# Three projection units instead of two beside the arriving input, with places of their own for their second weight halves

## The chip, the cores and the metric

The kernel runs on one NeuronCore of a Trainium2 chip. Five engines work side by side, each through its own list of instructions in order, and wait for one another by semaphores: TensorE (PE, matrix products; PEld is its loading of the stationary operand), VectorE (DVE), ScalarE (ACT), GpSimd (POOL), and SyncE (SP), which here only starts transfers (DMAs) from memory. The metric is the device time of one execution in microseconds (us); lower is better. Three runs of the kernel before gave 1511.23, 1511.27 and 1512.3 us, a median of 1511.27 us.

## The reference

One layer of a hybrid encoder trunk on x of 256 tokens by 2048 features, in float32. The part at issue is the very first: RMS norm of x, then one wide projection, whose first columns are the queries and keys of an attention with four heads of 128.

```python
u = _rms_norm(x, norm_mix_pre[l])           # x / rms(x) * gain
proj = u @ w_in                              # w_in: 2048 x 12580
sb, fox, rw, gates = _split(proj, ...)
q_a, k_a, v_a = _split(sb, (SB_WIDTH,) * 3)  # 512 columns each: four heads of 128
...                                          # attentions, time mixing, gates, output projection
x = x + _rms_norm(mix, norm_mix_post[l])
hdn = jnp.square(jax.nn.relu(_rms_norm(x, norm_mlp_pre[l]) @ w_mlp_up[l]))
x = x + _rms_norm(hdn @ w_mlp_down[l], norm_mlp_post[l])
```

## The kernel before

**Products in split form.** Float32 operands are cut into a rounded high part and the remainder as low part; ACT makes the high part by a copy, DVE the low part by a subtraction. A product then is high times (high, low) and low times high. For the features of x this gives a tile `xpk` of 128 x 512 (256 tokens high, 256 low) for each of 16 groups of 128 features, with the gain of the norm multiplied in. The factor 1/rms is left out at first and multiplied into the results later (`scaled`), so that the products need not wait for the norm.

**Units.** A unit is 128 output columns. Its weights are 2048 x 128, stored as two blocks of 128 x 1024 (512 KB): the first half holds feature groups 0 to 7, the second 8 to 15. Blocks come in the order of the array `wst`, so unit u has blocks 2u and 2u+1. Each block lands in a tile `raw` (tag `raw`, three places), is cut into `whi` (ACT) and `wlo` (DVE; three places each), and used by 8 products with the high part (128 x 512) and 8 with the low part (128 x 256). A unit adds up in one of four PSUM tiles `gps`.

**The ordinary loop.** `unit` (with `wnext`, `wraw` and `wsplit`) does one unit after another: load a block, cut it, multiply; the weights of the next block are made while TensorE works on the present one.

**The beginning.** x comes from memory in eight pieces of two feature groups (256 KB, `xload`), so TensorE cannot have all of xpk at once. For this time an order written out by hand holds on PE, ACT and DVE (`tc.manual_schedule`): two units, u = 0 and 1, are worked on together, feature group by feature group, as the pieces land. `part` cuts half a first block (512 columns), `xsplit` one feature group of x; `high` and `low` are the products; `whole` cuts a second block. SP issues all loads from one list, and an entry that waits holds back all behind it. The four raw blocks lie in four places: three of the tag `raw`, the fourth in a buffer of the tag `m`, which is used much later otherwise. Cut weights lie in the ordinary places of `whi` and `wlo`.

**After the beginning.** From here PE's order is still the written one, while ACT and DVE are ordered by the framework's scheduler. Units 2 to 7 follow in the ordinary loop (L191, L195 and L197 are their products). Between them ACT squares x (`square`, eight times 128 x 512, result in the tile `A6` of the tag `b6`), DVE adds the squares up (seven times), and behind the fifth unit TensorE sums them over the partitions (`norm`, L433). Then 1/rms is made, and the normed x is cut again for the later units.

Of the kernel before, what the change touches and what calls it, by code (L numbers as in the profile page):

```python
# [11 lines left out]
F32 = mybir.dt.float32  # L12
F32R = mybir.dt.float32r
AF = mybir.ActivationFunctionType
ALU = mybir.AluOpType
# [3 lines left out]
T = 256  # L19
# [4 lines left out]
HALF = 1024  # L24
# [28 lines left out]
def hybrid_block(ctx, tc, xt, x, gains, params, consts, lora, gup, wst, out):  # L53
    nc = tc.nc
    V, A, G, PE = nc.vector, nc.scalar, nc.gpsimd, nc.tensor

    cpool = ctx.enter_context(tc.tile_pool(name="cpool", bufs=1))
    wpool = ctx.enter_context(tc.tile_pool(name="wpool", bufs=1))
# [90 lines left out]
    wpos = [0]  # L149
# [5 lines left out]
    wq = []  # L155
# [4 lines left out]
    def wraw(n=None):  # L160
        raw = wpool.tile([128, HALF], F32, tag="raw", name=nm("raw"), bufs=3)
        rawdma[0] = nc.sync.dma_start(out=raw, in_=wst[wpos[0] if n is None else n])
        if n is None:
            wpos[0] = jump.get(wpos[0], wpos[0] + 1)
        return raw
# [4 lines left out]
    def wsplit(raw, n=None, now=True):  # L170
        hl = home[0](n) if home[0] else None
        hi, lo = hl or (wpool.tile([128, HALF], F32R, tag=t, name=nm(t), bufs=3) for t in ("whi", "wlo"))
        A.activation(hi, raw, AF.Copy)  # L173
        wq.append((hi, lo))
        low = lambda: V.tensor_tensor(lo, raw, hi.bitcast(F32), ALU.subtract)  # L175
        return low() if now else low
# [96 lines left out]
    rp = p1.enter_context(tc.tile_pool(name="rp", bufs=1))  # L273
# [17 lines left out]
    def xload(a, b):  # L291
        nc.sync.dma_start(out=X0[:, a:b, :], in_=xt[:, a:b, :])


    raws = {n: wpool.tile([128, HALF], F32, tag="raw", name=nm("raw"), bufs=3) for n in (0, 2)}
    for c in (0, 512):
        for n in (0, 2):
            nc.sync.dma_start(out=raws[n][:, c:c + 512], in_=wst[n][:, c:c + 512])
# [21 lines left out]
    ps = mps()  # L320
# [16 lines left out]

    def high(u, *ks):
        for k in ks:
            PE.matmul(qb[u], w[u, k // 8][0][:, k % 8 * 128:k % 8 * 128 + 128], xpk[k], start=k == 0, stop=False)  # L340

    def low(u, *ks):
        for k in ks:
            PE.matmul(qb[u][:, 0:T], w[u, k // 8][1][:, k % 8 * 128:k % 8 * 128 + 128], xpk[k][:, 0:T], start=False,
                      stop=k == 15)

    qb = [gps() for _ in range(2)]
    w = {(u, 0): [wpool.tile([128, HALF], F32R, tag=t, name=nm(t), bufs=3) for t in ("whi", "wlo")] for u in range(2)}

    def part(u, c, lo):  # L350
        c = slice(c, c + 512)
        hi, raw = w[u, 0][0][:, c], raws[2 * u][:, c]
        if lo:
            V.tensor_tensor(w[u, 0][1][:, c], raw, hi.bitcast(F32), ALU.subtract)
        else:
            A.activation(hi, raw, AF.Copy)

    def both(u, *ks):
        high(u, *ks)
        low(u, *ks)  # L360

    for c in (0, 512):
        k = c // 128
        part(0, c, False)
        xsplit(k)
        xsplit(k + 1)
        part(1, c, False)
        high(0, k, k + 1)
        high(1, k, k + 1)
        part(0, c, True)  # L370
        if c == 0:
            part(1, c, True)
        low(0, k, k + 1)
        xsplit(k + 2)
        xsplit(k + 3)
        if c:
            part(1, c, True)
        low(1, k, k + 1)
        both(0, k + 2, k + 3)
        both(1, k + 2, k + 3)  # L380

    def whole(n):
        later = wsplit(raws.pop(n), None, False)
        return wq.pop(), later

    w[0, 1], later = whole(1)
    xsplit(8)
    xsplit(9)
    later()
    both(0, 8, 9)  # L390
    xsplit(10)
    xsplit(11)
    both(0, 10, 11)
    w[1, 1], later = whole(3)
    later()
    both(1, 8, 9, 10, 11)
    for k in (12, 14):
        xsplit(k)
        xsplit(k + 1)
        both(0, k, k + 1)  # L400
        both(1, k, k + 1)
# [14 lines left out]
    side.append(lambda: const(ones, consts[:, 128:128 + NR]))  # L416
    side.append(rounded)
    side.append(lambda: const(con, consts[:, 128 + NR:]))
    wpos[0] = 4
    rstd = rp.tile([128, T], F32, tag="cs", name="rstd1", bufs=1)  # L420

    def square(i):
        xf = X0[:, 2 * i:2 * i + 2, :]
        b = 2 + 2 * (i % 2) if i else 0
        with tc.issue_after(behind[0].ins):
            A.activation(A6[:, b:b + 2, :], xf, AF.Square)
        if i:
            V.tensor_tensor(A6[:, 0:2, :], A6[:, 0:2, :], A6[:, b:b + 2, :], ALU.add)

    def norm():  # L430
        ps = mps()
        for i in range(2):
            PE.matmul(ps[:, 0:T], C("ones"), A6[:, i, :], start=i == 0, stop=i == 1)  # L433
        ms, t = tmp(), tmp()
# [37 lines left out]
    def later(i):  # L472
        normed(9 + i)
        if i < 5:
            scaled(i)
# [493 lines left out]
    for br in ("sb", "fox"):  # L969
        for s in ("q", "k"):  # L970
# [3 lines left out]
            for h in range(4):  # L974
                ps = unit(upk)
                t = g1()
# [5 lines left out]
        for i, nme, n in ((0, "zx", 128), (1, "zy", 128)) if br == "fox" else ((2, "zz", 36),):  # L982
            ps = unit(upk)
# [39 lines left out]
    for g in range(4):  # L1023
        m = rp.tile([128, 2, 512], F32, tag="m", name=nm("m"), bufs=4)
# [170 lines left out]
    low = more(False)  # L1195
# [312 lines left out]
    for g in range(4):  # L1508
        gs = slice(512 * g, 512 * g + 512)
        for tt, ps in enumerate(tok(hp, 4 if g == 3 else 1)):  # L1510
# [8 lines left out]
            if g == 3:  # L1519
                for c, w in (0, 512), (512, 512), (1024, 512), (1536, 256), (1792, 256):  # L1520
# [3 lines left out]
                        out=out[tt * 128:tt * 128 + 128, cs], in_=x1[tt][:, cs])  # L1524
# [125 lines left out]
```

## Time and profile before

| what | value |
|---|---|
| median of three runs | 1511.27 us |
| the profiled execution | 1512.76 us |
| its span in the trace | 1510.9 us |
| granted TensorE clock | 0.998 |
| busy in the span | PE 1492.3 us, PEld 1252.7, DVE 1207.6, ACT 939.4, POOL 94.6 |
| the two units done together: first product, end | 5.83 us, 21.46 us |
| the third unit (ordinary loop) | 21.46 to 27.05 us |
| the products of the norm | 38.23 us |

The profile's times count from the start of the span. A timeline row gives start, duration, engine, line, operation, result and operands, shape and how many; in square brackets stands the idle time of the engine just before it and what ended it. A transfer is issued by SP (rows SPq), and a view of the transfers gives size and time from issue to landing; the landing counts when the last of the 16 DMA engines is done.

### The profile page before, as it was taken

What the parts mean: (1) busy time and instruction counts of PE and PEld (TensorE: products, weight loads), DVE (VectorE), ACT (ScalarE), POOL (GpSimd) and SP (SyncE); (2) the same over time, 40 slices, a digit from 0 to 9 for tenths busy, and PEclk for the clock granted to TensorE, in tenths of its full rate; (3) what the DMA queues carried; (4) which work ended last, traced back from release to release, by engine and by line L of the source; (5) the groups of instructions that cost most, each with busy time, mean ns of one, the idle gap of its engine ahead of it and who ended that gap; (6) DMA issues with size and microseconds to landing.
All of it is one profiled execution on the core that took longest, in us unless ns stands there. A gap on an engine that the chain in (4) does not pass through costs nothing.

```text
span 1510.9 us, 22695 instructions
## 1 busy us (share of the span) xinstructions
PE 1492.3 (99%) x8384; PEld 1252.7 (83%) x8384; DVE 1207.6 (80%) x1673; ACT 939.4 (62%) x1433; POOL 94.6 (6%) x151
## 2 busy tenths in 40 slices
PE   9999999999999999999999999999999999999997
PEld 7888888887787887778888988888888888888886
DVE  7875679895678896476656778999899989999996
ACT  7665677545676445564445767677667666766663
POOL 0031003000002000000000000000000000000000
PEclk9999999999999999999999999999999999999999
DMA  7645455455444455355675758879888888889874
GB/s 266 196 168 182 141 180 162 148 179 187 134 170 166 155 190 174 127 182 193 214 245 172 253 178 252 251 220 287 258 262 235 222 274 240 270 265 255 251 222 150
DMA packets 104687, 312.71 MB, mean 207 GB/s; under 512 B 10240, under 2 KB 12288, under 8 KB 104576
## 3 DMA queue, kind: packets, MB, share of 16 engines
q1 hardware_dynamic: 93968, 279.87, 55.1%
q0 software_dynamic: 8064, 29.36, 10.4%
q10 hardware_dynamic: 2544, 2.03, 0.5%
q8 instruction: 66, 1.08, 0.3%
q14 instruction: 45, 0.37, 0.1%
HBM read 279.77 MB, written 2.10 MB: 187 GB/s over the span
## 4 chain that ended last, share of the span: by engine, by line
PE 94%; DVE 2%; issue 1%; ACT 1%; DMA 1%; DVEq 0%; POOLq 0%; POOL 0%; ACTq 0%; SPq 0%
PE gps L235 26%; PE gps L191 23%; PE gps L195 13%; PE gps L220 7%; PE mps L1368 3%; PE mps L1370 3%; PE mps L1369 3%; PE gps L1370 2%; PE gps L1368 2%; PE gps L1369 2%; PE gps L197 2%; DVE wlo L175 1%; PE mps L777 1%; PE gps L1157 1%; DMA raw<-in_wst_dram 1%
## 5 line engine op out<-in xcount | busy, mean ns | idle before, releaser
L175 DVE TENSOR_TENSOR wlo<-raw,whi 128x1024 fp32r<-128x1024 f32 x576 | 697.0, 1220 | 160.5 <-ACT whi L173 149.2
L173 ACT ACTIVATE whi<-raw 128x1024 fp32r<-128x1024 f32 x576 | 603.9, 1057 | 251.9 <-PE gps L235 85.8
L191 PE MATMUL gps<-pk,whi 128*128 128x512 f32 x1479 | 375.3, 392 | 0.5 <-DVE tmp L1286 0.3
L191 PEld LDWEIGHTS gps<-pk,whi 128*128 128x128 f32 x1479 | 274.4, 188 | 56.1 <-ACT whi L173 0.9
L235 PE MATMUL gps<-whi,pk 128*128 128x512 f32 x1004 | 254.8, 393 | 1.4 <-ACT whi L173 1.3
L195 PEld LDWEIGHTS gps<-pk,wlo 128*128 128x128 f32 x1582 | 215.6, 190 | 15.2 <-DVE wlo L175 0.3
L235 PEld LDWEIGHTS gps<-whi,pk 128*128 128x128 f32 x1004 | 186.1, 188 | 42.6 <-ACT whi L173 2.2
L195 PE MATMUL gps<-pk,wlo 128*128 128x256 f32 x1582 | 221.0, 282 | 0.0
L235 PE MATMUL gps<-wlo,pk 128*128 128x512 f32 x502 | 137.8, 393 | 1.7 <-DVE wlo L175 1.7
L235 PEld LDWEIGHTS gps<-wlo,pk 128*128 128x128 f32 x502 | 93.2, 188 | 22.4 <-DVE wlo L175 2.9
L1368 PE MATMUL mps<-whi,fm 128*128 128x512 f32 x224 | 88.6, 396 | 1.9 <-ACT whi L173 1.7
L1285 ACT ACTIVATE tmp<-gps 128x256 f32<-128x256 f32 x64 | 24.6, 384 | 102.9 <-PE gps L197 101.0
L1369 PE MATMUL mps<-whi,fm 128*128 128x512 f32 x224 | 87.7, 392 | 0.0
L1370 PE MATMUL mps<-wlo,fm 128*128 128x512 f32 x224 | 87.4, 390 | 0.0
L1348 POOL DMA_DIRECT2D raw<-raw x56 | 48.8, 872 | 572.4 <-DVE raw L1345 271.9
L1345 DVE TENSOR_TENSOR raw<-raw,raw 128x1024 f32<-128x1024 f32 x56 | 68.4, 1221 | 0.8
L1368 PE MATMUL gps<-whi,fm 128*128 128x512 f32 x168 | 65.9, 392 | 0.0
L1370 PE MATMUL gps<-wlo,fm 128*128 128x512 f32 x168 | 65.8, 391 | 0.0
L1369 PE MATMUL gps<-whi,fm 128*128 128x512 f32 x168 | 65.5, 390 | 0.0
L220 PE MATMUL gps<-whi,pk 128*128 128x512 f32 x224 | 60.7, 393 | 0.0
L1368 PEld LDWEIGHTS mps<-whi,fm 128*128 128x128 f32 x224 | 42.4, 189 | 10.0 <-ACT whi L173 4.0
L1370 PEld LDWEIGHTS mps<-wlo,fm 128*128 128x128 f32 x224 | 42.1, 188 | 9.5
(346 smaller groups left out, 1725.1 us busy)
## 6 DMA issues: line engine op xcount, KB each, us to landing
raw<-in_wst_dram SPq DMA_DIRECT2D x516, 512.0 KB, 4.4
raw<-raw POOLq DMA_DIRECT2D x56, 512.0 KB, 7.3
x<-in_xt_dram SPq DMA_DIRECT2D x8, 256.0 KB, 6.8
x<-in_x_dram SPq DMA_DIRECT2D x8, 256.0 KB, 5.1
raw<-in_wst_dram SPq DMA_DIRECT2D x4, 256.0 KB, 4.8
g<-in_gains_dram SPq DMA_DIRECT2D x4, 256.0 KB, 5.0
pk<-in_gains_dram SPq DMA_DIRECT2D x4, 256.0 KB, 6.9
out_dram<-x SPq DMA_DIRECT2D x4, 256.0 KB, 2.8
```

The costliest lines, as they stand in the source:

```text
L173: A.activation(hi, raw, AF.Copy)
L175: low = lambda: V.tensor_tensor(lo, raw, hi.bitcast(F32), ALU.subtract)
L191: PE.matmul(ps, hi[:, i * 128:i * 128 + 128], pks[i], start=first and i == 0, stop=False)
L195: PE.matmul(ps[:, 0:T], lo[:, i * 128:i * 128 + 128], pks[i][:, 0:T], start=False, stop=False)
L197: PE.matmul(ps, hi[:, (n - 1) * 128:n * 128], pks[n - 1], start=False, stop=True)
L220: PE.matmul(ps[tt], pks[k][:, c:c + 128], w[:, (k - k0) * 512:(k - k0) * 512 + 512], start=k == 0 and part == 0 and w is hl[0], stop=w is ...
L235: PE.matmul(ps[tt], pks[k][:, c:c + 128], w[:, (k - k0) * 512:(k - k0) * 512 + 512], start=k == 0 and part == 0 and w is hl[0], stop=False)
L1345: V.tensor_tensor(R[d, a], R[d, a], R[d, b], ALU.add)
L1348: G.dma_start(out=R[d, a], in_=R[d, b], accum_op=ALU.add)
L1368: PE.matmul(Q[f], a, w, start=d == d0 and i == 0, stop=False)
L1369: PE.matmul(Q[f], b, w, start=False, stop=False)
L1370: PE.matmul(Q[f], a, wl, start=False, stop=d == dn and i == 1)
```

## The change

Three units instead of two share the arriving pieces of x. The loads of the first halves of units 0, 1 and 2 are cut into two pieces of 512 columns each and interleaved with the pieces of x. They fill the three places of the tag `raw`. The three second halves (blocks 1, 3 and 5) are then loaded by `wraw` into the same three places, each followed by a piece of x, and their cut parts do not go to `whi` and `wlo` but to six tiles of their own: four of the tag `m`, one of `b6` and one of `Ti`. So `A6`, which is the only other tile of the tag `b6` at this stage, is taken after the group and not before it. The ordinary loop begins with unit 3 at block 6; the third unit is no longer done by it.

```diff
-    A6 = rp.tile([128, 6, T], F32, tag="b6", name="a6", bufs=1)
...
-    raws = {n: wpool.tile([128, HALF], F32, tag="raw", name=nm("raw"), bufs=3) for n in (0, 2)}
-    for c in (0, 512):
-        for n in (0, 2):
-            nc.sync.dma_start(out=raws[n][:, c:c + 512], in_=wst[n][:, c:c + 512])
-            xload(c // 128 + n, c // 128 + n + 2)
-    raws[1] = wraw(1)
-    xload(8, 10)
-    xload(10, 12)
-
-    raws[3] = rp.tile([128, 2, 512], F32, tag="m", name="raw3", bufs=4).rearrange("p a b -> p (a b)")
-    nc.sync.dma_start(out=raws[3], in_=wst[3])
-    xload(12, 14)
+    raws = {u: wpool.tile([128, HALF], F32, tag="raw", name=nm("raw"), bufs=3) for u in range(3)}
+
+    def wload(u, c):
+        nc.sync.dma_start(out=raws[u][:, c:c + 512], in_=wst[2 * u][:, c:c + 512])
...
+    seconds = []
+    for u in range(3):
+        seconds.append(wraw(2 * u + 1))
+        xload(8 + 2 * u, 10 + 2 * u)
     xload(14, 16)
...
+    more2 = [rp.tile([128, HALF], F32R, tag=t, name=nm("w2"), bufs=n) for t, n in
+             (("m", 4), ("m", 4), ("m", 4), ("m", 4), ("b6", 1), ("Ti", 1))]
...
+    def whole(u):
+        w[u, 1] = more2[2 * u:2 * u + 2]
+        A.activation(w[u, 1][0], seconds[u], AF.Copy)
+        return lambda: V.tensor_tensor(w[u, 1][1], seconds[u], w[u, 1][0].bitcast(F32), ALU.subtract)
...
+    part(2, 512, False)
+    part(2, 512, True)
+    both(1, 4, 5, 6, 7)
+    lo0 = whole(0)
+    lo0()
+    two(8)
+    both(2, 4, 5, 6, 7)
+    both(0, 8, 9)
+    lo1 = whole(1)
+    lo1()
+    two(10)
+    both(0, 10, 11)
+    both(1, 8, 9, 10, 11)
+    lo2 = whole(2)
+    lo2()
+    two(12)
+    both(2, 8, 9, 10, 11)
+    two(14)
+    for k in (12, 14):
+        for u in range(3):
+            both(u, k, k + 1)
...
-    wpos[0] = 4
+    wpos[0] = 6
+    A6 = rp.tile([128, 6, T], F32, tag="b6", name="a6", bufs=1)
...
-        ps = qb[h] if h < 2 else unit(xpk)
+        ps = qb[h] if h < 3 else unit(xpk)
```

How instructions stand now, at three places. The first is SP's list of loads at the start. Before, from the third load of weights on (`raw_88` and `raw_89` are the first halves of units 0 and 1, `raw_98` and `raw_102` the second halves, `x_82` is x, 128 x 512 is one piece of 256 KB):

```order
L298 DMA raw_88<-in_wst_dram 128x512
L292 DMA x_82<-in_xt_dram 128x512
L298 DMA raw_89<-in_wst_dram 128x512
L292 DMA x_82<-in_xt_dram 128x512 [waits DMAHW0_49]
L162 DMA raw_98<-in_wst_dram 128x1024 [waits DMAHW1_49]
L292 DMA x_82<-in_xt_dram 128x512 [waits DMAHW2_49]
L292 DMA x_82<-in_xt_dram 128x512 [waits DMAHW3_49]
L305 DMA raw_102<-in_wst_dram 128x1024 [waits DMAHW4_49]
```

Now, from the same third piece on (`raw_87`, `raw_88`, `raw_89` are the first halves of units 0, 1, 2; `raw_100`, `raw_103`, `raw_106` the second halves):

```order
L297 DMA raw_87<-in_wst_dram 128x512
L291 DMA x_82<-in_xt_dram 128x512
L297 DMA raw_88<-in_wst_dram 128x512 [waits DMAHW0_49]
L291 DMA x_82<-in_xt_dram 128x512 [waits DMAHW1_49]
L297 DMA raw_89<-in_wst_dram 128x512 [waits DMAHW2_49]
L162 DMA raw_100<-in_wst_dram 128x1024 [waits DMAHW6_49,DMAHW3_49,DVE_49]
L291 DMA x_82<-in_xt_dram 128x512 [waits DMAHW4_49]
L162 DMA raw_103<-in_wst_dram 128x1024 [waits DMAHW5_49,DMAHW0_49,DVE_49]
L291 DMA x_82<-in_xt_dram 128x512
L162 DMA raw_106<-in_wst_dram 128x1024 [waits DMAHW7_49,DMAHW2_49,DVE_49]
L291 DMA x_82<-in_xt_dram 128x512
```

Each second half now waits for DVE (DVE_49), which it did not before, and every later piece of x stands behind such a load.

The second place is DVE's list where the second halves come in. Before (`wlo_130` is the low part of unit 1's first half, `wlo_196` and `wlo_220` those of the second halves):

```order
L354 TENSOR_TENSOR wlo_130<-raw_89,whi_129 128x512 [waits DMAHW7_49]
L260 SCALAR_TENSOR_TENSOR xpk_198<-x_82,par,xpk_198 128x256 [waits DMAHW2_49,Activation_49]
L260 SCALAR_TENSOR_TENSOR xpk_201<-x_82,par,xpk_201 128x256 [waits Activation_49]
L175 TENSOR_TENSOR wlo_196<-raw_98,whi_195 128x1024 [waits DMAHW1_49]
L260 SCALAR_TENSOR_TENSOR xpk_209<-x_82,par,xpk_209 128x256 [waits DMAHW3_49,Activation_49]
L260 SCALAR_TENSOR_TENSOR pk_212<-x_82,par,pk_212 128x256 [waits Activation_49]
L175 TENSOR_TENSOR wlo_220<-raw_102,whi_219 128x1024 [waits DMAHW4_49,PE_49,Activation_49]
```

Now (`wlo_133` and `wlo_137` are low parts of first halves, `w_19_139` and `w_21_141` those of second halves in places of their own):

```order
L362 TENSOR_TENSOR wlo_133<-raw_87,whi_132 128x512 [waits DMAHW6_49,Activation_49]
L260 SCALAR_TENSOR_TENSOR xpk_188<-x_82,par,xpk_188 128x256 [waits DMAHW7_49,Activation_49]
L260 SCALAR_TENSOR_TENSOR xpk_191<-x_82,par,xpk_191 128x256 [waits Activation_49]
L362 TENSOR_TENSOR wlo_135<-raw_88,whi_134 128x512 [waits DMAHW0_49,Activation_49]
L260 SCALAR_TENSOR_TENSOR xpk_200<-x_82,par,xpk_200 128x256 [waits DMAHW1_49,Activation_49]
L260 SCALAR_TENSOR_TENSOR xpk_203<-x_82,par,xpk_203 128x256 [waits Activation_49]
L362 TENSOR_TENSOR wlo_137<-raw_89,whi_136 128x512 [waits DMAHW2_49,Activation_49]
L377 TENSOR_TENSOR w_19_139<-raw_100,w_18_138 128x1024 [waits DMAHW3_49,Activation_49]
L260 SCALAR_TENSOR_TENSOR xpk_222<-x_82,par,xpk_222 128x256 [waits DMAHW4_49,Activation_49]
L260 SCALAR_TENSOR_TENSOR xpk_225<-x_82,par,xpk_225 128x256 [waits Activation_49]
L377 TENSOR_TENSOR w_21_141<-raw_103,w_20_140 128x1024 [waits DMAHW5_49,Activation_49]
```

The low part of a second half stood behind the two feature groups that arrived with it and now stands ahead of them; the first low part in the list, `wlo_133`, is what frees the place of `raw_87`.

The third place is DVE's list behind the group. Before, the additions of squares (`a_83`) began ahead of the end of the two units, whose sums are taken over by L250:

```order
L260 SCALAR_TENSOR_TENSOR pk_248<-x_82,par,pk_248 128x256 [waits Activation_49]
L428 TENSOR_TENSOR a_83<-a_83 128x512 [waits Activation_49]
L175 TENSOR_TENSOR wlo_293<-raw_290,whi_292 128x1024 [waits DMAHW7_49,PE_49,Activation_49]
L428 TENSOR_TENSOR a_83<-a_83 128x512 [waits DVE_49,Activation_49]
L250 TENSOR_TENSOR g_48_281<-gps_125,tmp_282 128x256 [waits Activation_49]
```

Now the seven additions (`a_310`) all stand behind the three sums, the last of them between the two low parts of the sixth unit (`wlo_441`, `wlo_480`):

```order
L250 TENSOR_TENSOR g_60_337<-gps_131,tmp_338 128x256 [waits Activation_49]
L450 TENSOR_TENSOR a_310<-a_310 128x512 [waits DVE_49,Activation_49] x2
L175 TENSOR_TENSOR wlo_419<-raw_416,whi_418 128x1024 [waits DMAHW0_49,PE_49,Activation_49]
L450 TENSOR_TENSOR a_310<-a_310 128x512 [waits DVE_49,Activation_49] x3
L250 TENSOR_TENSOR g_72_403<-gps_348,tmp_404 128x256 [waits Activation_49]
L450 TENSOR_TENSOR a_310<-a_310 128x512 [waits DVE_49,Activation_49]
L175 TENSOR_TENSOR wlo_441<-raw_438,whi_440 128x1024 [waits DMAHW1_49,Activation_49]
L450 TENSOR_TENSOR a_310<-a_310 128x512 [waits DVE_49,Activation_49]
L175 TENSOR_TENSOR wlo_480<-raw_477,whi_479 128x1024 [waits DMAHW2_49,PE_49,Activation_49]
```

Behind the norm the order of ACT, DVE, POOL, SP and PE is the same as before.

More of the change, by code (lines that the diff above doesn't have):

```diff
@@ L292, in xload @@
         nc.sync.dma_start(out=X0[:, a:b, :], in_=xt[:, a:b, :])
-    raws = {n: wpool.tile([128, HALF], F32, tag="raw", name=nm("raw"), bufs=3) for n in (0, 2)}
-    for c in (0, 512):
-        for n in (0, 2):
-            nc.sync.dma_start(out=raws[n][:, c:c + 512], in_=wst[n][:, c:c + 512])
-            xload(c // 128 + n, c // 128 + n + 2)
-    raws[1] = wraw(1)
-    xload(8, 10)
-    xload(10, 12)
-    raws[3] = rp.tile([128, 2, 512], F32, tag="m", name="raw3", bufs=4).rearrange("p a b -> p (a b)")
-    nc.sync.dma_start(out=raws[3], in_=wst[3])
-    xload(12, 14)
+    raws = {u: wpool.tile([128, HALF], F32, tag="raw", name=nm("raw"), bufs=3) for u in range(3)}
+    def wload(u, c):
+        nc.sync.dma_start(out=raws[u][:, c:c + 512], in_=wst[2 * u][:, c:c + 512])
+    wload(0, 0)
+    xload(0, 2)
+    wload(1, 0)
+    wload(2, 0)
+    xload(2, 4)
+    wload(0, 512)
+    xload(4, 6)
+    wload(1, 512)
+    xload(6, 8)
+    wload(2, 512)
+    seconds = []
+    for u in range(3):
+        seconds.append(wraw(2 * u + 1))
+        xload(8 + 2 * u, 10 + 2 * u)
     xload(14, 16)
@@ L345, in low @@
                       stop=k == 15)
-    qb = [gps() for _ in range(2)]
-    w = {(u, 0): [wpool.tile([128, HALF], F32R, tag=t, name=nm(t), bufs=3) for t in ("whi", "wlo")] for u in range(2)}
+    qb = [gps() for _ in range(3)]
+    w = {(u, 0): [wpool.tile([128, HALF], F32R, tag=t, name=nm(t), bufs=3) for t in ("whi", "wlo")] for u in range(3)}
+    more2 = [rp.tile([128, HALF], F32R, tag=t, name=nm("w2"), bufs=n) for t, n in
+             (("m", 4), ("m", 4), ("m", 4), ("m", 4), ("b6", 1), ("Ti", 1))]
     def part(u, c, lo):
         c = slice(c, c + 512)
-        hi, raw = w[u, 0][0][:, c], raws[2 * u][:, c]
+        hi, raw = w[u, 0][0][:, c], raws[u][:, c]
         if lo:
@@ L360, in both, with two @@
         low(u, *ks)
-    for c in (0, 512):
-        k = c // 128
-        part(0, c, False)
+    def two(k):
         xsplit(k)
         xsplit(k + 1)
[L367 to L389, printed above, removed]
+    def whole(u):
+        w[u, 1] = more2[2 * u:2 * u + 2]
+        A.activation(w[u, 1][0], seconds[u], AF.Copy)
+        return lambda: V.tensor_tensor(w[u, 1][1], seconds[u], w[u, 1][0].bitcast(F32), ALU.subtract)
+    part(0, 0, False)
+    two(0)
+    part(0, 0, True)
+    part(1, 0, False)
+    high(0, 0, 1)
+    part(1, 0, True)
+    high(1, 0, 1)
+    part(2, 0, False)
+    low(0, 0, 1)
+    low(1, 0, 1)
+    part(2, 0, True)
+    both(2, 0, 1)
+    two(2)
+    for u in range(3):
+        both(u, 2, 3)
+    part(0, 512, False)
+    part(0, 512, True)
+    two(4)
+    part(1, 512, False)
+    part(1, 512, True)
+    both(0, 4, 5)
+    two(6)
+    both(0, 6, 7)
+    part(2, 512, False)
[5 more added lines that the diff above has]
+    both(2, 4, 5, 6, 7)
     both(0, 8, 9)
-    xsplit(10)
-    xsplit(11)
+    lo1 = whole(1)
+    lo1()
+    two(10)
     both(0, 10, 11)
-    w[1, 1], later = whole(3)
-    later()
     both(1, 8, 9, 10, 11)
+    lo2 = whole(2)
[3 more added lines that the diff above has]
+    two(14)
     for k in (12, 14):
[L398 to L401, printed above, removed]
+        for u in range(3):
+            both(u, k, k + 1)
     order.__exit__(None, None, None)
```

## Prediction

> **What bounds the kernel now.** I read the page's shares first, then the busy time by stage, with cuts at the two borders that the change moves: the end of the two units done together and the end of the third.
>
> ```profile
> span 1510.9 us, 22695 instructions
> PE 1492.3 (99%) x8384; PEld 1252.7 (83%) x8384; DVE 1207.6 (80%) x1673; ACT 939.4 (62%) x1433; POOL 94.6 (6%) x151
> ...
> 0.00:21.46 21.46, 18.14 (x76) 13.69 (x77) 13.89 (x28) 15.91 (x31) 0.76 (x12) 1.00 0.85 301
> 21.46:27.05 5.59, 5.59 (x34) 4.92 (x33) 5.18 (x8) 4.73 (x8) 0.00 (x0) 1.00 0.65 209
> 27.05:1510.90 1483.85, 1468.59 (x8277) 1234.11 (x8275) 1188.49 (x1638) 918.79 (x1396) 93.85 (x139) 1.00 0.66 206
> ```
>
> TensorE is the bound: busy 1492.3 of 1510.9 us, and without a gap in the third unit, which takes 5.59 us there. All units have the same products, so the only thing to win is idle time ahead of 21.46. TensorE's timeline shows it:
>
> ```profile
> 5.83 1.36 PE L340 MATMUL gps<-xpk,whi 128*128 128x512 f32 x4
> 8.84 0.90 PE L340 MATMUL gps<-xpk,whi 128*128 128x512 f32 x2 [0.90 <-DVE xpk L260]
> 13.28 0.51 PE L344 MATMUL gps<-xpk,wlo 128*128 128x256 f32 x2 [0.80 <-DVE wlo L354]
> 21.46 2.00 PE L191 MATMUL gps<-xpk,whi 128*128 128x512 f32 x8
> 23.30 1.12 PE L195 MATMUL gps<-xpk,wlo 128*128 128x256 f32 x8
> 24.25 0.86 PE L191 MATMUL gps<-xpk,whi 128*128 128x512 f32 x3
> 27.05 2.00 PE L191 MATMUL gps<-xpk,whi 128*128 128x512 f32 x8
> 38.23 1.02 PE L433 MATMUL mps<-a,cr 128*128 128x256 f32 x4
> ```
>
> Eight high products issue in 1.84 us (21.46 to 23.30), eight low ones in 0.95: 0.23 and 0.12 each, so 0.70 for a pair of feature groups in one unit. Two units without waits would end at 5.83 + 2 x 5.59 = 17.01; they end at 21.46. So 4.45 us are lost to waits, and that is the most the change can win. Its mark is 27.05, where three units are done now. If three units end at E, the kernel moves by E - 27.05, as long as TensorE then runs on without a new gap.
>
> What the waits hang on is the arrival of the pieces. The issues, then four of their landings (size, us from issue to landing):
>
> ```profile
> 1.65 0.42 SPq L298 DMA_DIRECT2D raw<-in_wst_dram  x1
> 2.59 0.43 SPq L298 DMA_DIRECT2D raw<-in_wst_dram  x1
> 3.54 0.43 SPq L298 DMA_DIRECT2D raw<-in_wst_dram  x1
> 4.54 0.73 SPq L162 DMA_DIRECT2D raw<-in_wst_dram  x1
> ...
> raw<-in_wst_dram SPq DMA_DIRECT2D x1, 256.0 KB, 3.7
> raw<-in_wst_dram SPq DMA_DIRECT2D x1, 256.0 KB, 5.8
> raw<-in_wst_dram SPq DMA_DIRECT2D x1, 256.0 KB, 6.9
> raw<-in_wst_dram SPq DMA_DIRECT2D x1, 512.0 KB, 7.8
> ```
>
> The third piece of 256 KB lands at 1.65 + 3.7 = 5.4, the fifth at 2.59 + 5.8 = 8.4, the seventh at 10.4, the second half at 12.3. ACT's waits give the fourth and the sixth, since it starts on x as it lands:
>
> ```profile
> 7.75 0.91 ACT L259 ACTIVATE xpk<-x,par 128x256 fp32r<-128x256 f32 x2 [1.58 <-DMA x<-in_xt_dram]
> 9.80 0.91 ACT L259 ACTIVATE xpk<-x,par 128x256 fp32r<-128x256 f32 x2 [0.62 <-DMA x<-in_xt_dram]
> 10.62 0.61 ACT L356 ACTIVATE whi<-raw 128x512 fp32r<-128x512 f32 x1
> 12.35 1.06 ACT L173 ACTIVATE whi<-raw 128x1024 fp32r<-128x1024 f32 x1 [0.32 <-DMA raw<-in_wst_dram]
> 11.14 0.68 DVE L354 TENSOR_TENSOR wlo<-raw,whi 128x512 fp32r<-128x512 f32 x1
> 11.74 0.87 DVE L260 SCALAR_TENSOR_TENSOR xpk<-x,par,xpk 128x256 fp32r<-128x256 f32 x2
> 14.65 1.22 DVE L175 TENSOR_TENSOR wlo<-raw,whi 128x1024 fp32r<-128x1024 f32 x1
> 15.78 0.48 DVE L260 SCALAR_TENSOR_TENSOR xpk<-x,par,xpk 128x256 fp32r<-128x256 f32 x1
> ```
>
> So: fourth 7.7, fifth 8.4, sixth 9.8, seventh 10.4. The second half, two sizes behind the eighth piece, lands 1.9 us after the seventh: 0.64 for each 256 KB while the queue is full. The rows also price the cutting: a half of a first block 0.61 on ACT and 0.68 on DVE, a block 1.06 and 1.22 (the next starts 1.13 after it), two feature groups 0.91 and 0.88.
>
> **The change, part by part.**
>
> *First halves of three units.* The queue's first ten pieces are now, in order: weights 0, x 0-1, weights 1, weights 2, x 2-3, weights 0, x 4-5, weights 1, x 6-7, weights 2 (0, 1, 2: the unit). Same sizes, so I put them at the landings above: weights 2 at 7.7, x 2-3 at 8.4, the second piece of weights 0 at 9.8, x 4-5 at 10.4, then 11.1, 11.7, 12.4. Against before, x comes one place later. TensorE starts at 5.83 as before, ends units 0 and 1 of groups 0-1 at 7.7, waits 0.8 for weights 2 (ACT 7.76 to 8.37) and 0.3 for their low part; groups 2-3 (x landed 8.4, ACT to 9.3, DVE to 9.9, in which the low part of weights 2 stands ahead) cost two waits of 0.17, groups 6-7 (DVE 13.0 and 13.4) 0.57 and 0.17. With 0.5 at weights 1 and the first groups the loss is 2.6, and half of the work, 8.4 us, is done at 5.83 + 8.4 + 2.6 = 16.8.
>
> *Second halves.* A second half now goes into the place of a first half, so SP issues it only when DVE has cut that one. For unit 0: landed 9.8, ACT to 10.4, DVE to 11.14, issue 11.2; before, SP issued the first of them at 4.54, with no wait on DVE. Units 1 and 2 in the same way: DVE is done with their first halves at 12.6 and 14.0. Behind each waits a piece of x, up to the last at 14.8. By 12.4 all that was queued has landed, so the queue runs dry and the flight from issue to landing, hidden before, shows. Its price stands where the loads come alone:
>
> ```profile
> raw<-in_wst_dram SPq DMA_DIRECT2D x14, 512.0 KB, 3.8
> ...
> raw<-in_wst_dram SPq DMA_DIRECT2D x1, 512.0 KB, 3.2
> ...
> raw<-in_wst_dram SPq DMA_DIRECT2D x1, 512.0 KB, 5.0
> ```
>
> These are the 14 block loads issued from 20 to 60 us, and two single ones, at 49.35 and at 21.14. The middle is 3.8, the ends 3.2 and 5.0. I take 3.8: the first second half lands at 15.0. The rest follows at 0.64 per 256 KB, because it is issued in time: x 8-9 at 15.65, second half of unit 1 at 16.9, x 10-11 at 17.6, unit 2 at 18.8, x 12-13 at 19.5, x 14-15 at 20.1.
>
> [...]
>
> *The chain behind it.* ACT cuts unit 0's second half from 15.05 to 16.1. DVE works its list in order: low part 16.14 to 17.36, groups 8 and 9 to 17.76 and 18.16, low part of unit 1 (ACT done 18.0) to 19.30, groups 10 and 11 to 19.70 and 20.10. TensorE, done with first halves at 16.8, waits 1.1 + 0.17 for groups 8 and 9 and 1.1 + 0.17 for 10 and 11. After group 11 (20.10, and 0.15 to start) it has left: one high and two low products (0.47), groups 8-11 of units 1 and 2 (2.8), groups 12-15 of three units (6 x 0.70 = 4.2). Group 15 is cut at 22.8, in time. E = 20.25 + 7.4 = 27.65.
>
> *Work that grows.* Unit 2's first half is cut in two pieces (ACT 2 x 0.61 for 1.06, DVE 2 x 0.68 for 1.22, one more DMA). On DVE this lies in the chain, and I counted it. POOL has none of it.
>
> *Squares behind the group.* A6 is free only when unit 2's last product is done. Before, additions ran up to here, 7 us ahead of the norm's products:
>
> ```profile
> 19.30 0.69 DVE L428 TENSOR_TENSOR a<-a 128x512 f32<-128x512 f32 x1
> 21.64 0.42 DVE L250 TENSOR_TENSOR g<-gps,tmp 128x256 f32<-128x256 f32 x1
> 30.55 0.68 DVE L428 TENSOR_TENSOR a<-a 128x512 f32<-128x512 f32 x1
> ```
>
> Now DVE has, between E and the norm (two units, 11.18 us later, as 38.23 is after 27.05): four sums of 0.42, three low parts of 1.22, seven additions of 0.69 = 10.2 us. It begins with some of it before E. I cost this at nothing; the cover is these two units, and only about 1 us of it is spare. If a low part in this list comes late, the norm's products wait, at most 1.5 us by that list plus an ACT copy ahead of it.
>
> *Later.* The order behind the norm is unchanged, so the shift stays.
>
> *The sum.* Waits lost before 4.45, now 2.6 + 2.45 = 5.05: +0.6 us on the profiled span of 1510.9, which makes 1511.5. That execution took 1512.76, 1.49 above the median of 1511.27, so the median goes to 1511.9. The loss at the queue eats what sharing x wins. Ends of the unknowns: the flight from 3.2 to 5.0 gives E 27.0 to 28.8. The landings four to ten hang on a slow stage early on (the fourth piece 2.3 us behind the third, against 0.64 later); a us less there makes E a us earlier, 0.5 more is as likely. Together E 26.0 to 29.3, 1510.2 to 1513.5.
>
> **The rivals.** *The overlap works as written:* second halves come so early that TensorE never waits after 5.83: E = 5.83 + 3 x 5.59 = 22.6, -4.45, 1506.8. For it: the queue moved a block in 1.3 us while full. Against: three waits of SP on DVE, and the first half's own waits of 2.6.
>
> *The second halves fly as long as those of the full queue:* 7.1 to 7.8 us, not 3.8 (the row at 4.54 had 7.8). Place: SP's first load that waits on DVE. E = 27.65 + 3.3 to 4.0, slower by 3.9 to 4.6, 1515.2 to 1515.9. It decides from a flight of 6.2 on, where E passes 30.1. Against: by the landings above some six pieces stood ahead of that row, here hardly one does. For: all landings are those of the slowest engine, and the load at 21.14 took 5.0 with an empty queue.
>
> *The norm comes late:* DVE's list of 10.2 us does not fit: up to 1.5 us more, 1513.4, still within 0.2%.
>
> **How the numbers follow.** 0.2% is 3.0 us, about what a measurement of this kernel can tell from no change. The forecast (E 26.0 to 29.3) 0.75; the late norm 0.04, also no change; the long flight 0.14, slower; the full overlap 0.07, faster. The time is the forecast's, 1511.9, its own range 1510.2 to 1513.5. For 8 in 10 the range must take in part of the long flight: 1509.8 to 1515.4.
>
> **What would show it.** SP's first load of 512 KB issued at about 11.2, behind a wait on DVE; ACT's first cut of a whole block at 15.0 (it was 12.35); TensorE idle about 1.1 us twice between 16.8 and 20.3; the first L191 products at 27.65; no idle time at the norm's products. A first L191 ahead of 26 would say that the landings were mis-sized, behind 30 that the flight was; a gap at the norm that the squares were.

## The result, and the profile after

The changed kernel took 1514.75 us in the median of 21 runs (1511.57 to 1517.53), the kernel before 1511.95 us in 21 runs: a ratio of 1.0016, 95% interval 1.001 to 1.0022. So it is about 2.4 us slower by the ratio (the medians lie 2.8 us apart), 0.16%, which is still inside the 0.2% that the prediction took as no change. The forecast was +0.6 us. The sign holds, and so does the wide range of 1509.8 to 1515.4, which took in part of a rival; the forecast's own range, 1510.2 to 1513.5, does not. The size is four times too small, and a part of it is something that the forecast did not have at all.

The profiled execution took 1514.82 us, with a span of 1513.0 (2.1 more than before). First the page's totals and the busy time by stage (in the stage rows: start and end, length, busy time of PE, PEld, DVE, ACT and POOL, granted TensorE clock, DMA share, GB/s). The cuts are the first product, the end of the first halves, the second wait, the end of the slow products, and the end of the three units.

```profile
span 1513.0 us, 22702 instructions
PE 1494.1 (99%) x8384; PEld 1255.3 (83%) x8384; DVE 1208.8 (80%) x1674; ACT 939.7 (62%) x1434; POOL 94.6 (6%) x151
...
5.74:15.57 9.83, 9.80 (x48) 7.59 (x48) 7.86 (x15) 7.15 (x14) 0.00 (x0) 1.00 1.01 313
15.57:19.86 4.29, 1.14 (x5) 0.68 (x5) 2.48 (x6) 2.68 (x4) 0.00 (x0) 0.82 0.87 329
19.86:25.39 5.53, 5.53 (x17) 4.61 (x18) 4.39 (x8) 4.44 (x9) 0.00 (x0) 0.52 0.96 316
25.39:30.10 4.71, 4.71 (x30) 4.18 (x29) 1.47 (x2) 1.24 (x3) 0.00 (x0) 1.00 0.74 253
```

The products are the same as before, yet PE is busy for 1.8 us more (1494.1 for 1492.3): a first sign that some of them ran slowly. The stages say where. In the first halves TensorE counts as busy almost throughout, though their products are only 8.4 us of work by the prediction's prices: short waits hide in this count. Then TensorE worked 1.14 of 4.29 us, and after that it was busy for 5.53 us at a granted clock of 0.52. Finer cuts show where the half clock begins and ends:

```profile
15.57:18.33 2.76, 1.14 (x4) 0.67 (x4) 0.95 (x4) 1.24 (x2) 0.00 (x0) 1.00 0.77 281
18.33:25.16 6.83, 5.30 (x16) 4.42 (x17) 5.74 (x9) 5.68 (x10) 0.00 (x0) 0.50 0.98 337
25.16:30.04 4.88, 4.88 (x30) 4.31 (x29) 1.65 (x2) 1.39 (x4) 0.00 (x0) 1.00 0.75 259
```

It lasts 6.83 us and begins at 18.33, while TensorE still waits. TensorE's timeline of the changed kernel shows the same as single groups (L346 and L350 are now `high` and `low`, L191 the ordinary loop, L455 the norm):

```profile
5.74 1.36 PE L346 MATMUL gps<-xpk,whi 128*128 128x512 f32 x4
...
14.94 0.63 PE L350 MATMUL gps<-xpk,wlo 128*128 128x256 f32 x4
16.03 0.90 PE L346 MATMUL gps<-xpk,w 128*128 128x512 f32 x2 [0.46 <-DVE xpk L260]
16.77 0.40 PE L350 MATMUL gps<-xpk,w 128*128 128x256 f32 x2
19.86 0.79 PE L346 MATMUL gps<-xpk,w 128*128 128x512 f32 x1 [2.69 <-DVE xpk L260]
...
21.30 1.48 PE L346 MATMUL gps<-xpk,w 128*128 128x512 f32 x3
...
23.86 1.46 PE L346 MATMUL gps<-xpk,w 128*128 128x512 f32 x3
...
30.04 2.00 PE L191 MATMUL gps<-xpk,whi 128*128 128x512 f32 x8
...
41.22 1.02 PE L455 MATMUL mps<-a,cr 128*128 128x256 f32 x4
```

Two waits, of 0.46 and 2.69 us, both on `xpk`; the second is from 17.17 to 19.86. Behind it, in the group at 21.30, a high product issues every 0.43 us and not every 0.23 (three of them from 21.30 to the next group at 22.58). The mark, the first L191 product, is at 30.04: 2.99 us later than the 27.05 of before. No idle time stands at the norm.

What TensorE waited for shows in SP's issues, two landings of 512 KB (the load issued at 9.66, then the one at 11.21), ACT's cuts of the second halves (L376) and DVE's (L377):

```profile
9.66 0.33 SPq L162 DMA_DIRECT2D raw<-in_wst_dram  x1
...
11.21 0.33 SPq L162 DMA_DIRECT2D raw<-in_wst_dram  x1
...
12.61 0.33 SPq L162 DMA_DIRECT2D raw<-in_wst_dram  x1
...
raw<-in_wst_dram SPq DMA_DIRECT2D x1, 512.0 KB, 3.6
...
raw<-in_wst_dram SPq DMA_DIRECT2D x1, 512.0 KB, 5.9
...
13.27 1.06 ACT L376 ACTIVATE w<-raw 128x1024 fp32r<-128x1024 f32 x1 [1.48 <-DMA raw<-in_wst_dram]
...
17.09 1.06 ACT L376 ACTIVATE w<-raw 128x1024 fp32r<-128x1024 f32 x1 [1.97 <-DMA raw<-in_wst_dram]
...
18.18 1.23 DVE L377 TENSOR_TENSOR w<-raw,w 128x1024 fp32r<-128x1024 f32 x1 [1.81 <-ACT w L376]
```

The second half of unit 0 landed at 13.3, that of unit 1 only at 11.21 + 5.9 = 17.1. ACT and DVE take things in the order written, so groups 10 and 11, which DVE makes behind the low part of unit 1, were ready only near 20, and they are what the next products in TensorE's list need.

### The profile page after: what moved, and what is told of

Its sections match the earlier page's. It is cut to its first block, busy times and chain, and to the rows that moved or that the text cites. A ratio compares the mean times of both kernels' runs of the same rounds, so it can differ in the third digit from the quotient of the medians.

```text
span 1513.0 us, 22702 instructions
## 1 busy us (share of the span) xinstructions
PE 1494.1 (99%) x8384; PEld 1255.3 (83%) x8384; DVE 1208.8 (80%) x1674; ACT 939.7 (62%) x1434; POOL 94.6 (6%) x151
## 4 chain that ended last, share of the span: by engine, by line
PE 90%; DVE 5%; issue 2%; DMA 1%; ACT 1%; SPq 0%; DVEq 0%; POOLq 0%; POOL 0%; ACTq 0%
PE gps L235 23%; PE gps L191 22%; PE gps L195 12%; PE gps L220 7%; PE mps L1390 3%; PE mps L1392 3%; PE mps L1391 3%; PE gps L1392 2%; PE gps L1390 2%; PE gps L1391 2%; DVE wlo L175 2%; PE gps L197 2%; DMA raw<-in_wst_dram 1%; DVE Ti L846 1%; DVE tp L844 1%
## 5 line engine op out<-in xcount | busy, mean ns | idle before, releaser
L191 PE MATMUL gps<-pk,whi 128*128 128x512 f32 x1475 | 374.1, 392 | 0.2 <-ACT whi L173 0.2
L191 PEld LDWEIGHTS gps<-pk,whi 128*128 128x128 f32 x1475 | 273.9, 188 | 55.1 <-ACT whi L173 0.9
```

The lines of the kernel that those rows point to most:

```text
L191: PE.matmul(ps, hi[:, i * 128:i * 128 + 128], pks[i], start=first and i == 0, stop=False)
```

## Experiments

Two questions stood open. Is it the wait of the second halves for the places of `raw` that costs, or something else in sharing among three units? And is the half clock a consequence of idle TensorE time, or an accident of this one execution? Theory A says the place and the idle time. Rival B says that sharing itself, the cutting of blocks or the added work costs, and that idle time costs its own length only. Rival C, in some of the expectations, says that the products behind the wait are slow from something else in these 5 us, such as the transfers or the cutting. Each ratio is to the kernel before on the same chip, with its 95% interval.

### Second halves in places of their own

The changed kernel with each second half loaded as two pieces of 512 columns into tiles of the tag `pk`, which are free at this stage. SP then waits for no compute engine ahead of these loads.

```diff
-        seconds.append(wraw(2 * u + 1))
+        seconds.append([pk().bitcast(F32) for _ in range(2)])
+        for i, s in enumerate(seconds[u]):
+            rawdma[0] = nc.sync.dma_start(out=s, in_=wst[2 * u + 1][:, 512 * i:512 * i + 512])
         xload(8 + 2 * u, 10 + 2 * u)
...
-        A.activation(w[u, 1][0], seconds[u], AF.Copy)
-        return lambda: V.tensor_tensor(w[u, 1][1], seconds[u], w[u, 1][0].bitcast(F32), ALU.subtract)
+        hi, lo = ([t[:, c:c + 512] for c in (0, 512)] for t in w[u, 1])
+        for h, s in zip(hi, seconds[u]):
+            A.activation(h, s, AF.Copy)
...
+            for h, l, s in zip(hi, lo, seconds[u]):
+                V.tensor_tensor(l, s, h.bitcast(F32), ALU.subtract)
```

> The changed kernel, but each second half is loaded in two pieces of 512 columns into free buffers of the tag pk, so that SP waits for no engine before it issues them; the rest of the order stays. Theory A (the wait of SP for a place of the tag raw runs the queue dry, and TensorE's gap and its slow products follow from that): all of x is in by 17 to 19 us, no gap of TensorE over 1.3 us, granted clock 1.00 from 10 us on, first L191 products at 24.9 to 26.3 instead of 30.0, and a time 1 to 2 us under the kernel before. Rival B (the three units together are limited by ACT's and DVE's cutting, and the late loads are hidden behind it): first L191 products still behind 28, time as the changed kernel's, about 2.4 us over the kernel before.

Measured: 1509.2 us (1508.43 to 1511.73, 11 runs), ratio 0.9985 (0.9977 to 0.9994). It is faster than both kernels. From its trace: SP's first load of a second half, TensorE's only idle time from there to the mark, the mark, and the two stages in which the changed kernel lost its time.

```profile
5.68 0.97 SPq L313 DMA_DIRECT2D pk<-in_wst_dram  x2
...
12.13 0.90 PE L348 MATMUL gps<-xpk,whi 128*128 128x512 f32 x2 [0.39 <-DVE xpk L260]
...
24.69 2.00 PE L191 MATMUL gps<-xpk,whi 128*128 128x512 f32 x8
...
6.03:15.90 9.87, 9.48 (x50) 7.79 (x49) 9.04 (x18) 8.82 (x19) 0.00 (x0) 1.00 1.03 361
15.90:24.69 8.79, 8.79 (x50) 7.39 (x49) 6.92 (x13) 6.62 (x14) 0.00 (x0) 1.00 0.98 366
```

The issue moves from 9.66 to 5.68, TensorE is never idle behind 15.90, the clock stays at 1.00, and the mark comes at 24.69, 2.36 before that of the kernel before. Mark and gain (2.5 us in the medians) are a little better than expected. Sharing among three units is therefore a gain in itself. But this edit also cuts the blocks in two, so it does not yet say which of its two parts did it.

### The same cut in the same places, and the places of their own again

```diff
-        seconds.append([pk().bitcast(F32) for _ in range(2)])
+        place = wpool.tile([128, HALF], F32, tag="raw", name=nm("raw"), bufs=3)
+        seconds.append([place[:, c:c + 512] for c in (0, 512)])
```

This is the kernel above with one thing put back: the pieces land in the places of `raw`, so that SP waits for DVE again. Both ran side by side.

> The changed kernel with each second half loaded and cut in two pieces of 512 columns, as in the version with places of their own, but landing in the three places of the tag raw, so that SP still waits for DVE. Theory A (what costs is the wait for the place): issues stay at about 9.7, 11.2 and 12.6 us; the cut alone wins at most 1.0 us, since ACT can start on a piece 0.6 us before the other lands and the last step on DVE is 0.68 and not 1.22 us; first L191 at 26.0 to 27.5 where the granted clock stays up, 28 to 30 where it falls; 1511.0 to 1514 us, not faster than the kernel before. Rival B (cutting the blocks was the gain, the place nothing): first L191 at 24.7, 1509 us, faster by 0.15%.

> The version with places of their own once more, on the same chip as its neighbour. Theory A: first L191 at 24.5 to 25.0 us, 1509.2 us, faster than the kernel before by 0.1 to 0.2%, and faster than the cut in the same places by 2 to 5 us. Rival B: level with the cut in the same places.

Measured: 1514.17 us (1512.16 to 1518.09, 12 runs), ratio 1.001 (1.0001 to 1.0019), for the cut in the same places; 1509.91 us (1508.83 to 1512.91, 11 runs), ratio 0.9982 (0.9973 to 0.999), for the places of their own. Nothing but the place differs, and it is worth 4.3 us, the half clock included. The profiled execution of the places of their own (1511.19 us) had its mark at 25.46, behind the 24.5 to 25.0 expected and 1.59 ahead of the kernel before. That is 0.8 us behind the first trace, and stands already at the end of the first halves (16.68 and 15.90); it was not traced further. From the trace of the cut in the same places, SP's first issue, ACT's wait for the next piece of x, TensorE and two stages:

```profile
9.61 0.80 SPq L314 DMA_DIRECT2D raw<-in_wst_dram  x2
...
16.68 0.91 ACT L259 ACTIVATE xpk<-x,par 128x256 fp32r<-128x256 f32 x2 [2.77 <-DMA x<-in_xt_dram]
...
17.77 1.09 PE L349 MATMUL gps<-xpk,w 128*128 128x512 f32 x2 [2.20 <-DVE xpk L260]
...
19.89 0.79 PE L349 MATMUL gps<-xpk,w 128*128 128x512 f32 x1 [0.61 <-DVE xpk L260]
...
30.04 2.00 PE L191 MATMUL gps<-xpk,whi 128*128 128x512 f32 x8
...
15.50:19.90 4.40, 1.59 (x6) 0.93 (x5) 2.64 (x6) 3.21 (x7) 0.00 (x0) 0.82 1.07 385
19.90:25.50 5.60, 5.60 (x17) 4.68 (x18) 4.45 (x9) 4.91 (x9) 0.00 (x0) 0.53 0.94 358
```

Here a piece of x, issued at 10.46, is the late one (landed near 16.7), and the wait is split differently, 2.20 and 0.61. The waits add up to 2.81 us (3.15 in the changed kernel), and the mark of 30.04 is the same. The half clock, too, is the same: worked out from the clocks of these two stages (0.82 and 0.53), it is granted from about 18.3 to 25.2, though here TensorE had been at work since 17.77 when it began. Mark and time lie just above what was expected (28 to 30 with the fall, 1511.0 to 1514 us). Whether the cut alone won anything, the runs cannot tell: its ratio of 1.001 and the changed kernel's 1.0016 have intervals that overlap. Rival B falls.

### The kernel before with one made wait

To test idle time alone, the kernel before computes the low part of unit 0's second half two, three or four times into the same tile (the values are the same each time). TensorE then waits there, and nothing of the change is in it.

```diff
-    later()
+    for i in range(2):
+        later()
```

> The kernel before, with the low part of unit 0's second half computed twice, so that TensorE waits for it 1.25 us longer (about 1.5 us in all, at 16 us); nothing else is moved. Theory A with a border between 1.5 and 2.7 us: first L191 products at 22.7, 1.25 us later, no row at half clock, time +1.25. If the clock falls already here: first L191 products at 24 or later, time +2.5 or more.

> The kernel before, with the low part of unit 0's second half computed four times, so that TensorE waits 3.8 us longer (about 4 us in all); no transfer is moved. Theory A (half speed follows an idle TensorE): first L191 products at 25.2 plus 2 to 2.7 us, so 27.2 to 27.9, time +5.8 to +6.5. Rival C (the slow products of the changed kernel come from something else): 25.2, time +3.8.

> The kernel before, with the low part of unit 0's second half computed three times: TensorE idle 2.8 us in one piece at 15 to 18 us, about as long as in the changed kernel. Between 1.5 us (no half clock) and 4.1 us (half clock for 5.3 us). Theory A: half clock as in the changed kernel, first L191 products at 23.9 plus 2 to 2.7 us, time +4.5 to +5. If the border lies between 2.8 and 4.1 us: 23.9, time +2.5, and the changed kernel's fall of the clock needs its second, shorter gap too.

Measured: twice, 1513.8 us (10 runs), ratio 1.0012 (1.0002 to 1.0021); three times, 1514.76 us (10 runs), 1.0019 (1.001 to 1.0028); four times, 1517.85 us (4 runs), 1.0041 (1.0028 to 1.0055). The waits and the marks (here the end of the two units, 21.46 before) in the three traces, twice first:

```profile
17.28 0.51 PE L344 MATMUL gps<-xpk,wlo 128*128 128x256 f32 x2 [1.53 <-DVE wlo L175]
...
22.83 1.99 PE L191 MATMUL gps<-xpk,whi 128*128 128x512 f32 x8
```

Three times, with the stage behind the wait:

```profile
17.99 0.51 PE L344 MATMUL gps<-xpk,wlo 128*128 128x256 f32 x2 [2.79 <-DVE wlo L175]
...
23.55 2.00 PE L191 MATMUL gps<-xpk,whi 128*128 128x512 f32 x8
...
17.99:23.55 5.56, 5.56 (x31) 4.67 (x32) 5.46 (x10) 3.06 (x6) 0.00 (x0) 1.00 0.45 168
```

Four times, with the stage behind the wait:

```profile
18.91 0.80 PE L344 MATMUL gps<-xpk,wlo 128*128 128x256 f32 x2 [4.07 <-DVE wlo L175]
...
20.79 1.48 PE L340 MATMUL gps<-xpk,whi 128*128 128x512 f32 x3
...
26.65 2.00 PE L191 MATMUL gps<-xpk,whi 128*128 128x512 f32 x8
...
18.91:24.20 5.29, 5.29 (x16) 4.54 (x17) 5.20 (x9) 1.07 (x3) 0.00 (x0) 0.50 0.48 173
```

After 1.53 us and, in this execution, after 2.79 us the products behind the wait take as long as before: 5.55 us (17.28 to 22.83) and 5.56 us, 5.54 in the kernel before (15.92 to 21.46). After 4.07 us the clock is at 0.50 (from about 17.6 to 24.4, worked out from its means of 0.85 over 14.60 to 18.91 and 0.98 over 24.20 to 30.00): the same products took 5.56 us behind the wait of 2.79 (17.99 to 23.55), and 7.74 here (18.91 to 26.65), 2.2 us more. That is the half clock of the changed kernel, made in a kernel without the change. The times agree: by the ratios 1.8, 2.9 and 6.2 us over the kernel before, where 1.25, 2.5 (without a fall) and 5.8 to 6.5 (with one) were expected. A wait of 2.79 us in one piece without a fall is not what theory A expected.

With the wait of 2.79 us the mean clock over the whole span differs from execution to execution: 0.998 in two of ten (1513.37 and 1514.29 us), 0.997 in five, 0.996 or 0.995 in three (1514.89 to 1515.65). A fall of 6.83 us at half clock takes 0.002 off that mean (6.83 x 0.5 / 1513). In the traces of before and after the clock is also at half over the last 7.38 and 6.49 us of the span; before, which has no other fall, has a mean of 0.998, after, which has one, 0.996, and 0.997 decides nothing. With four times, all runs had 0.996 or 0.997. So with the wait of 2.79 us the fall probably came in some executions and not in others; the mean does not say where in the span it lay, and the one profile taken has none. With 4.07 us the one profiled has it.

### The wait filled with products

If the half clock comes from idle time, useless products in the wait should keep the clock up. In the changed kernel, products of zeros into a sum that nobody reads stand behind groups 8 and 9 of unit 0, first 20 of them, then 6.

```diff
     both(0, 8, 9)
+    for i in range(6):
+        PE.matmul(ps[:, 0:T], z[:, 0:128], z, start=True, stop=True)
     lo1 = whole(1)
```

> The changed kernel with 20 products of zeros (128 x 256, 0.12 us each, into a PSUM tile that nobody reads) behind unit 0's products with groups 8 and 9, where TensorE stands idle for 2.7 us. All arrivals stay as they are. Theory A (the products behind the gap run at half speed because TensorE was idle before): products of groups 10 and 11 issue every 0.23 us, granted clock 1.00 between 20 and 25 us, first L191 products about 27.4 instead of 30.0, time 2 to 2.6 us under the changed kernel, that is at most 0.5 us over the kernel before. Rival C (they are slow from something else that falls into these 5 us, such as the transfers or the cutting): they stay at 0.43 us, first L191 products at 30 or later, time as the changed kernel's or up to 1 us more.

> As the run with 20 products of zeros, but with 6, since each took 0.42 us and not 0.12 (two passes): 2.5 us of work in a gap of 2.7 us. Theory A: no row at half clock, first L191 products 27.2 to 27.8, time 2 to 2.6 us under the changed kernel run beside it, within 0.7 us of the kernel before. Rival C: first L191 products at 30 or later, time as the changed kernel's or more.

Measured: with 20, 1519.87 us (5 runs), ratio 1.0057 (1.0043 to 1.007); with 6, 1513.54 us (1511.92 to 1515.14, 11 runs), ratio 1.0008 (0.9999 to 1.0017). The fillings as they stand in the two traces, 20 first:

```profile
17.34 8.80 PE L411 MATMUL mps<-tmp 128*128 128x256 f32 x40
```

```profile
17.12 2.75 PE L411 MATMUL mps<-tmp 128*128 128x256 f32 x12
...
27.87 2.00 PE L191 MATMUL gps<-xpk,whi 128*128 128x512 f32 x8
...
19.80:25.30 5.50, 5.46 (x30) 4.58 (x30) 4.61 (x9) 4.58 (x9) 0.00 (x0) 1.00 0.94 282
```

The first was badly sized: a product of plain float32 appears as two entries and took 0.42 us, not 0.12, so 20 of them were 8.5 us of new work. With 6 the filling lay in the wait almost exactly, the granted clock was 1.00 through the stage that was slow before, and the mark came at 27.87 and not 30.04, although unit 1's second half landed as late as before (17.1). That speaks against rival C: the transfers and the cutting of the second halves were still there. All 11 executions had a mean clock of 0.997 or 0.998. The expected gain of 2 us and more over the changed kernel did not show in the run times: the median is level with that of the next experiment, which is the time that rival C had forecast. That the filling costs its own time in executions in which the load comes earlier is a likely reason (where the changed kernel keeps its clock, it takes 1512.19 us, see the next table), but was only argued.

### The changed kernel once more

> The changed kernel once more, beside the next one on the same chip. Theory A: TensorE's gap ahead of the products with groups 10 and 11 and the rows at half clock behind it come again, first L191 products at 28 to 31, time 2 to 3 us over the kernel before. If the first trace was an odd one (a single late load): no half clock, first L191 products near 27, time within 1 us of the kernel before.

Measured: 1513.42 us (1511.6 to 1518.01, 11 runs), ratio 1.0011 (1.0002 to 1.002). Its profiled execution did not show the fall:

```profile
16.80 0.89 PE L346 MATMUL gps<-xpk,w 128*128 128x512 f32 x2 [0.99 <-DVE xpk L260]
...
19.25 0.50 PE L346 MATMUL gps<-xpk,w 128*128 128x512 f32 x1 [1.33 <-DVE xpk L260]
...
27.23 2.00 PE L191 MATMUL gps<-xpk,whi 128*128 128x512 f32 x8
```

Here unit 1's second half flew 5.0 us and not 5.9, the waits were 0.99 and 1.33, and the mark is 27.23, 0.18 behind before. This is the mark that the expectation had for the case that the first trace was an odd one; the time (1.7 us over the kernel before by the ratio) is above the 1 us that it allowed then. The 32 executions of the changed kernel in both series, by their mean granted clock:

| mean clock over the span | executions | median, us |
|---|---|---|
| 0.998 | 7 | 1512.19 |
| 0.997 | 10 | 1514.12 |
| 0.995 or 0.996 | 15 | 1515.06 |

Where the mean clock is at 0.998, the changed kernel is level with the kernel before (1511.95). The slowdown goes with the lower means. That the fall at 18 us is what lowers them was seen in one profile only; but of the 71 executions of the kernel before in the series of the experiments 66 had 0.998 or more, and the other five took 1514.77 to 1516.57 us. The version with places of their own had 0.998 in 21 of its 22 executions.

## Why the prediction was right, and where it was not

**The verdict.** No change within 0.2% came true, in part by luck. The mark of 30.04 lies outside the forecast's 26.0 to 29.3 and behind the 30 that the prediction named as the sign of a mis-sized flight, just short of the 30.1 from which the rival of the long flight was to decide. Two errors, one late load and a cost that the sum did not have, were partly made good by a third, the early pieces.

**The bound and the mark.** Right as far as the two profiles show: the change acted at the start. Of the 2.99 us at the mark 2.1 are left in the span; the rest of the span was 0.9 us shorter than in before's profiled execution, and that 0.9 was not traced to a cause.

**First halves.** The landings of the early pieces were put too late. The prediction had first halves end at 16.8, they ended at 15.57, and with the first product 0.09 us earlier the loss there was 1.4 us (15.57 less 5.74 and 8.4 of work), not 2.6.

**SP waits for DVE, and the flight shows.** Right in kind, and this is the term that decides: with the place as the only difference, 4.3 us in the medians. The issues came at 9.66, 11.21 and 12.61, forecast at 11.2, 12.6 and 14.0. The first flight was 3.6 us, forecast 3.8.

**The next loads follow in time.** Wrong. The prediction let unit 1's second half land 1.9 us behind unit 0's, because it was issued in time. It landed 3.8 us behind, after a flight of 5.9 (5.0 in the second profile of the changed kernel). That 17.1 is close to the 16.9 of the prediction is luck: the issue was 1.4 us earlier than forecast, the flight 1.6 longer than the 4.3 that the forecast gave it. So the waits were 0.46 and 2.69 and not 1.1 with 0.17 twice (2.45 in the sum). This is the rival of the long flight in a milder form: 5.9 is just short of the 6.2 at which that rival was to decide; the third second half flew 6.4 (issued at 12.61, landed at 19.0), but TensorE did not wait for it. In the two fillings this load landed at 17.1 and 17.3, so it is no single accident. In the trace of the changed kernel 14 of the 16 DMA engines were done with it about 2 us ahead of the last two (by 15.1; 17.0 and 17.1). Why these two are late stays open; it was not tried.

**Idle TensorE costs its length.** This is the step that was missing. The sum priced a wait at its own time. In the profiled execution the second wait was followed by 5.53 us at a clock of 0.52, which is 5.53 x 0.48 = 2.65 us of lost work. In a kernel without the change the made wait of 4.07 us was followed by 5.29 us at 0.50; with six products in the wait, and in the second profile of the changed kernel, with waits of 0.99 and 1.33, the clock was 1.00 from 19.80 to 25.30. How much idle time takes the clock down was not shown: no wait of the changed kernel is longer than 2.69 us, and the clock fell at 18.33, when TensorE had been idle for 0.46 and then 1.16 us (17.17 to 18.33).

In the prediction's own sum, for the mark (which has a slip of 0.07 in it, as 0.47 + 2.8 + 4.2 is 7.47 and not 7.4): 27.65, less 0.09 for the earlier start, less 1.17 for the first halves, plus 0.70 for the waits (3.15 for 2.45), plus 2.65 for the clock, is 29.74; 30.04 was measured, and 0.3 is not assigned. No run shows the 0.15 us that the sum has TensorE start behind DVE: the second wait here ended 0.06 us behind it (19.80 to 19.86). Without the clock the errors nearly cancel, and an execution like that at 27.23 looks like a good forecast, which is luck too.

**The squares and the norm.** Right: no idle time at L455, 11.18 us behind the mark. DVE's last addition for it is done 1.6 us ahead:

```profile
38.96 0.68 DVE L450 TENSOR_TENSOR a<-a 128x512 f32<-128x512 f32 x1
```

**The rivals.** Full overlap did not come, for the reasons given against it; places of their own bring 2.36 of its 4.45 us. The late norm did not come.

## What to carry to other kernels

A prefetch into a place that must first be freed is not a prefetch: here the queue behind it ran dry (a DMA share of 0.30 from 10.00 to 10.50), and the next loads showed their flight, 3.6, 5.9 and 6.4 us, with the slowest of 16 DMA engines in it (in the second of them two came about 2 us behind the other 14). Look in the order of the issuing engine for a wait on a compute engine ahead of a load, and give that load a place that is already free; here this turned +2.4 us into -2.5. And price a wait of TensorE at its length, and look at the granted clock behind it: in the traces here a fall to half cost 2.2 to 2.7 us more. It came with waits of 4.07, of 0.46 and 2.69, and of 2.20 and 0.61 us, and not with 1.53, with 2.79 in one piece, or with 0.99 and 1.33.

## What the runs showed of the hardware

- In the trace of the changed kernel the half clock lasted 6.83 us, 18.33 to 25.16. In the two others that show it, it lasted about 6.8 us, worked out from the clocks of their stages: about 18.3 to 25.2 with the cut blocks, 17.6 to 24.4 around the made wait of 4.07 us. The falls were worth 2.65 us (5.53 x 0.48), 2.6 (5.60 x 0.47) and 2.2 (7.74 less 5.56).
- The length of the longest wait did not decide alone: the made wait of 2.79 us passed without a fall in its profile, waits of 2.20 and 0.61 us had one, and in the changed kernel it came 1.16 us into the longer wait. The traces side by side:

| trace | waits of TensorE between 14 and 20 us | clock in a stage behind them |
|---|---|---|
| made wait, four times | 4.07 us | 0.50, 18.91 to 24.20 |
| changed kernel | 0.46 and 2.69 us | 0.52, 19.86 to 25.39 |
| cut in the same places | 2.20 and 0.61 us | 0.53, 19.90 to 25.50 |
| made wait, three times | 2.79 us | 1.00, 17.99 to 23.55 |
| changed kernel once more | 0.99 and 1.33 us | 1.00, 19.80 to 25.30 |
| six products in the wait | none (filled from 17.12 to 19.87) | 1.00, 19.80 to 25.30 |

With the made wait of 1.53 us the products behind it took 5.55 us, as against 5.54 before. What else decides whether a fall comes was not shown.
- In the filling with 20 a product of plain float32 (128 x 256) took two entries and 0.42 us together (20 of them from 17.34 to 25.79, in 40 entries), where a product of the rounded form of the same size issues in 0.12 (eight in 0.95 us, 23.30 to 24.25, in the kernel before).
